# One decoder layer on one core: the third output tile's weights split by halves, and turned attention probabilities copied bank by bank on two engines

## The chip, the cores and the metric

The kernel runs on one core of a Trainium2 chip. The metric is the device time of one execution in microseconds. Times of instructions come from one profiled execution, counted from its first instruction.

## What is computed

One layer of a hybrid decoder for 1024 tokens of width 1024, all in float32:

```python
h = rmsnorm(x, norm1_w)
proj = h @ w_in                       # columns are shared out between two mixers
o_a = gated_delta_rule(...)           # 4 heads of 128, after a short causal convolution
o_b = dilated_attention(qb, kb, vb)   # 8 heads of 64; three (window, dilation) branches
x = x + concat(o_a, o_b) @ w_out      # one output projection
h = rmsnorm(x, norm2_w)
u = causal_dwconv(h @ w_up, ffn_conv_w)
x = x + (silu(u[:, :2816]) * u[:, 2816:]) @ w_down
return rmsnorm(x, final_norm_w)
```

The attention lets each query see the last 128 keys, every fourth key of the last 512 and every sixteenth of the last 2048.

## The kernel before

**Precision.** A float32 product is made of three products of a reduced type (`mm3`, L196): both operands are split into a high part (a ScalarE copy into the reduced type) and a low part (VectorE subtracts the high part from the original). The products are high × high, high × low and low × high. `split` (L202) makes such a pair; `weight` (L211) takes a raw weight tile of 128 × 1024 (`wst`, loaded by DMA), allots `whi` and `wlo` from rings of two buffers each, and splits it; `wk` (L219) views the two as eight blocks of 128 columns, one for each block of the contraction.

**Order of the work.** The kernel is written as streams (Python generators). A planner, `Weave` (L46 to L118), runs them against a simple model of the engines: each call on VectorE or ScalarE is charged a fixed time and a time per column (L148 to L154), and a stream goes on when the tiles that it asks for (`need`) are ready by that model. So the planner fixes the order of TensorE's list. Dense products of the input projection have a low rank (level 9) and fill the places where other streams would wait. The order on the other engines is fixed when the program is built, by a scheduler that works with priorities. Engine handles `ve` and `ac` have the plain priority of their place in the program; `uv` and `ua` (L151, L152) take the same instructions with a precedence of 400 places (`URGENT`). Helpers record all instructions of these handles under one line: L139 for the plain ones, L141 for those with precedence; L189 is every matmul and L193 every transpose on TensorE.

**Banks.** Matmul results go to PSUM banks of 128 × 512, allotted from rings of two by tag (`asc`, `atr`, `hf`, `ch`).

**Attention** (L892 to L1043). Four pairs of heads, each with eight query blocks of 128, are worked off as 16 pairs of blocks. For a pair, `scores` makes query-key products in two banks for each block: near keys (128 columns for the first block, else 256) and far keys (32 columns for each earlier block before the neighbour, in `far` columns in all). `softmax` finds the minimum of the negated scores on VectorE (`mx`), exponentiates on ScalarE into `sm`, with the sums in `den`. `turn` (L942) transposes the probabilities in pieces of 64 queries: one bank for the first 64 queries, the other for the last 64 (`pvs`, `HALVES`). From each bank the near part (up to 2 heads × 2 × 64 columns) is copied into `pt`, where the two halves lie interleaved, and each far part (2 × 64 columns; none for the first two blocks, one for the next four, two for the last two) into `pb`. Then come the scores of the next pair, which need the same four banks, and `values`, which multiplies `pt` by the values. `rd` is the reciprocal of the sums, on VectorE.

**Output projection** (L1080 to L1120). Eight output tiles of 128 channels, in the order `MORDER` (L1049): 0, 4, 1, 5, 2, 6, 3, 7. The first two are built up together while the mixers' outputs arrive, one in `hf` banks and one in `ch` banks. The others follow one by one, two halves of 24 matmuls each, in `hf` banks. After a tile, VectorE adds its banks to the residual rows `x1` (the profile's `x`); then (L1113 to L1115) the weights of the tile after next are split and its residual rows are loaded, and `residual` (L1142) stores `x1` (to `xpark`) and makes the inputs of the up-projection (`hb`, `B`, `T`) and the sums of squares (`sq`, `rstdB`). DMAs are issued from one queue, SyncE's.

Of the kernel before, what the change touches and what calls it, by code (L numbers as in the profile page):

```python
# [7 lines left out]
F32 = mybir.dt.float32  # L8
F32R = mybir.dt.float32r
AF = mybir.ActivationFunctionType  # L10
OP = mybir.AluOpType
# [4 lines left out]
P = 128  # L16
S = 1024
KT = 8
# [126 lines left out]
def hybrid_layer(tc, I, out):  # L145
# [5 lines left out]
    uv = Engine(wv, nc.vector, "vector", 0.07, 0.00105, first=tc.high_priority)  # L151
    ua = Engine(wv, nc.scalar, "scalar", 0.12, 0.00085, first=tc.high_priority)  # L152
# [4 lines left out]
    wp = es.enter_context(tc.tile_pool(name="wp", bufs=1))  # L157
# [5 lines left out]
    def tile_(pool, shape, dt, name, tag, bufs):  # L163
        return wv.slot(pool.tile(list(shape), dt, name=name, tag=tag, bufs=bufs), tag, bufs)
# [3 lines left out]
    def A(name, tag, dt=F32, shape=(P, 1024)):  # L168
        if tag in TURNS:
            i = turns[tag] = turns.get(tag, -1) + 1  # L170
            tag = TURNS[tag][i % len(TURNS[tag])]
        return tile_(lp, shape, dt, name, tag, SLOTS[tag])
# [19 lines left out]
    def tp(dst, src, idt=None, us=0.11):  # L192
        tc.stamp_issue_order_token(nc.tensor.transpose(dst, src, ident if idt is None else idt).ins, TOKEN)  # L193
        wv.product(us, dst, src)

    def mm3(dst, lhs, rhs, first, last, **kw):  # L196
        us = 0.2135 * rhs[0].shape[-1] / 512
        mm(dst, lhs[0], rhs[0], us, first, False, **kw)
        mm(dst, lhs[0], rhs[1], us, False, False, **kw)
        mm(dst, lhs[1], rhs[0], us, False, last, **kw)  # L200

    def split(src, hi, lo):  # L202
        ac.activation(hi, src, AF.Copy)
        return ve.tensor_tensor(lo, src, hi.bitcast(F32), op=OP.subtract)

    def raw_weight(src, n=1024):
        st = tile_(wp, [P, n], F32, "wst", "wst", 2)
        sy.dma_start(st, src)
        return st

    def weight(src, n=1024, st=None):  # L211
        if st is None:
            st = raw_weight(src, n)
        hi = tile_(wp, [P, n], F32R, "whi", "whi", 2)
        lo = tile_(wp, [P, n], F32R, "wlo", "wlo", 2)
        split(st, hi, lo)
        return hi, lo

    def wk(src, st=None):  # L219
        return [t.rearrange("p (k m) -> p k m", k=KT) for t in weight(src, st=st)]  # L220
# [23 lines left out]
    def bank(tag, name="ps"):  # L244
        return tile_(pp_, (P, 512), F32, name, tag, 2)
# [7 lines left out]
    def half(i):  # L253
        return slice(i * 512, i * 512 + 512)
# [17 lines left out]
    for k in range(KT):  # L272
        xt = A("xt", ("kT*", "dv*")[k % 2])
        xts.append(xt)
        if k % 2 == 0:
            wst = tile_(wp, [P, 2, 384], F32, "wst", "wst", 2)
            whi, wlo = [A(nm, "uy", F32R, (P, 2, 384)) if k < 4 else A(nm, "kt", F32R, (P, 2, 384))
                        for nm in ("whi", "wlo")]
# [611 lines left out]
    HALVES = (slice(0, 64), slice(64, 128))  # L890

    def attention():  # L892
# [49 lines left out]
        def turn(pair):  # L942
            pts = A("pt", "dv*", shape=(P, 2, 2, 256))
            for b, (it, tag) in enumerate(zip(pair, ("asc", "atr"))):
                sm, near, far, u, den = it["sm"], it["near"], it["far"], it["u"], it["den"]
                nn, nf = near // P, -(-far // P)
                pt = it["pt"] = pts[:, b]
                pps = [bank(tag) for _ in range(2)]
                yield wv.need(*pps, sm, slack=TSLACK[b])
                pvs = [pp.rearrange("p (e i t) -> p e i t", e=2, t=64) for pp in pps]  # L950
                for e in range(2):
                    for i in range(nn + nf):
                        o = far + i * P if i < nn else (i - nn) * P
                        for pv, rr in zip(pvs, HALVES):
                            tp(pv[:, e, i, :], sm[rr, e, o:o + P], ident[rr, rr], 0.055)
                for pv, rr in zip(pvs, HALVES):
                    uv.tensor_copy(pt.rearrange("p e (i t) -> p e i t", t=P)[:, :, :nn, rr], pv[:, :, :nn, :])
                    for i in range(nf):
                        rows = min(it["far"] - i * P, P)
                        ua.activation(it["pb"][i][:rows, :, u, rr], pv[:rows, :, nn + i, :], AF.Copy)  # L960
                rd = it["rd"] = tile_(sp, [P, P], F32, "rd", ("r0", "r1", "w0", "w1")[u], 1)
                uv.reciprocal(rd.rearrange("p (e d) -> p e d", e=2), den[:, :, None].to_broadcast([P, 2, 64]))

# [62 lines left out]
        for pi in range(4):  # L1026
            q, k, vn, vc = cur
            for hh in range(2):
# [4 lines left out]
                pb = [A("pb", "qa", shape=(P, 2, 4, P)) for _ in range(1 + hh)]  # L1033
# [15 lines left out]
    MORDER = (0, 4, 1, 5, 2, 6, 3, 7)  # L1049

    def load_residual(m):
        x1[m] = A("x1", "kT")
        sy.dma_start(x1[m], I["xT"][m * P:(m + 1) * P, :])
# [26 lines left out]
    def out_proj():  # L1080
        yield from wv.until("dense")
        ws = [wk(I["wo"][m]) for m in MORDER[:2]]
        yield from wv.until("last group")
        yield from wv.until("residual")
        pts = {}
        todo = [(k, j) for k in range(8) for j in range(2)]
        while todo:

            now = [a for a in todo if ("ot", a[0]) in wv.done and (a[1] == 0 or "attention" in wv.done)]
            if not now:  # L1090
                yield 0.3
                continue
            k, j = now[0]
            todo.remove(now[0])
            m, w = MORDER[j], ws[j]
            if m not in pts:
                pts[m] = [bank(("hf", "ch")[j]) for _ in range(2)]
            for h in range(2):
                yield wv.need(pts[m][h], *w, *ots[k])
                mm3(pts[m][h], [t[:, k, :] for t in w], [t[:, half(h)] for t in ots[k]], k == 0, k == 7)  # L1100
        for j, m in enumerate(MORDER):
            w = ws.pop(0)
            for h in range(2):
                if j > 1:
                    pt = bank("hf")
                    yield wv.need(pt, *w)
                    for k in range(8):
                        mm3(pt, [t[:, k, :] for t in w], [t[:, half(h)] for t in ots[k]], k == 0, k == 7)
                        yield 0.0
                else:  # L1110
                    pt = pts[m][h]
                ve.tensor_tensor(x1[m][:, half(h)], x1[m][:, half(h)], pt, op=OP.add)
            if j + 2 < 8:  # L1113
                ws.append(wk(I["wo"][MORDER[j + 2]]))
                load_residual(MORDER[j + 2])  # L1115
            elif j == 6:
                up_first()
                wv.done.add("last weights")
            residual(m)
        wv.done.add("proj")  # L1120
# [21 lines left out]
    def residual(m):  # L1142

        sy.dma_start(xpark[m], x1[m])
        t = hb[m] = A("hb", "dv")
        for h in range(2):
            ac.activation(t[:, half(h)], x1[m][:, half(h)], AF.Copy, scale=n2[:, m:m + 1])
        i = m % 4
        if m < 4:
            split_block(hblock("B11", i), t[:, half(0)])  # L1150
            t1 = tile_(sp, [P, 512], F32, "t1s", "t2", 2)
            ve.tensor_tensor(t1, t[:, half(1)], t[:, half(0)], op=OP.subtract)
            split_block(hblock("T1", i), t1)
        else:
            (b11, b12), (b21, b22) = [[x[:, half(h)] for h in range(2)] for x in (hb[i], t)]

            ve.tensor_tensor(b12, b22, b12, op=OP.subtract)
            ve.tensor_tensor(b11, b12, b11, op=OP.add)
            split_block(hblock("T2", i), b11)
            split_block(hblock("B21", i), b21)  # L1160
            split_block(hblock("T3", i), b12)
            ve.tensor_tensor(b21, b21, b11, op=OP.subtract)
            split_block(hblock("T4", i), b21)
            split_block(hblock("B22", i), b22)
        for h in range(2):
            sl = half(h)
            sq = tile_(sp, [P, 512], F32, "sq2", "t2", 2)
            ac.activation(rstdB[:, sl] if m == 0 else sq, x1[m][:, sl], AF.Square)
            if m:
                ve.tensor_tensor(rstdB[:, sl], rstdB[:, sl], sq, op=OP.add)  # L1170
# [66 lines left out]
    def up_first():  # L1237
        load_up(0)
        up_weights(0, ("A11", "S1"))
# [271 lines left out]
    for h in range(H):  # L1511
        wv.add(1, chain(h))
    wv.add(5, attention())
    wv.add(8, out_proj())
    wv.add(0, mixer_splits())
    wv.add(8, mlp_up())
# [61 lines left out]
```

## Time and profile before

| | us |
|---|---|
| median of 3 runs | 1223.74 |
| lowest and highest | 1222.77, 1223.82 |
| the profiled execution | 1223.87 |
| its span, first to last instruction | 1222.1 |
| attention on TensorE | about 330 to 460 |
| output projection | about 481 to 570 |
| up-projection, then down-projection | to about 992, then to the end |

In the profile, PE is TensorE's matrix multiplication, PEld its loading of weights, DVE VectorE, ACT ScalarE, SP the DMA queue's engine. A row of a timeline gives the start, the time from start to end, the engine, the line, the operation, the tiles written and read, the shapes and the count, and in brackets the idle time of that engine before it with what ended it. A row of a group gives the count, the busy time in all in us, the mean of one in ns, and the idle time before. Matmuls overlap: a 128 × 512 product is shown as 0.39 us long though the next one starts 0.23 after it.

### The profile page before, as it was taken

The numbers are of one execution on the slowest core, as the hardware profiler recorded it, in microseconds if no ns is written. First come the engines' busy times: TensorE is split into PE (matmuls) and PEld (weight loads), VectorE is DVE, ScalarE is ACT, GpSimd is POOL, SyncE is SP. The second block draws the span as 40 slices with busy tenths as digits, with TensorE's granted clock in tenths as the row PEclk, the third lists the DMA queues.
The fourth block names the chain that finished last, engine by engine and source line by source line (L and its number), as shares of the span: only waits on it lengthen the run. The fifth ranks groups of instructions, "written<-read, shape, count | busy, mean of one in ns | idle before, by whom it ended". The sixth has DMA issues, their size and how long they took to land.

```text
span 1222.1 us, 18237 instructions
## 1 busy us (share of the span) xinstructions
PE 1201.4 (98%) x7064; PEld 986.3 (81%) x7064; DVE 950.3 (78%) x1458; ACT 574.5 (47%) x1123; POOL 50.1 (4%) x46
## 2 busy tenths in 40 slices
PE   9999999999999999999999999999999999999996
PEld 7878887889777778788888888888888888787886
DVE  7675965566487686668988988989889889899875
ACT  7393344356344453555545544445444444343441
POOL 0211010003100000000000000000000000000000
PEclk9999999999999999999999999999999999999998
DMA  7425252335634213444223123132231496555623
GB/s 228 110 74 168 77 148 88 118 126 163 215 105 121 88 37 101 157 147 155 71 68 104 58 98 99 57 104 65 91 101 55 142 369 238 165 164 181 193 81 138
DMA packets 85799, 154.81 MB, mean 127 GB/s; under 512 B 21168, under 2 KB 36304, under 8 KB 85712
## 3 DMA queue, kind: packets, MB, share of 16 engines
q1 hardware_dynamic: 85712, 153.64, 39.3%
q8 instruction: 55, 0.90, 0.3%
q14 instruction: 32, 0.26, 0.1%
HBM read 117.68 MB, written 35.93 MB: 126 GB/s over the span
## 4 chain that ended last, share of the span: by engine, by line
PE 84%; DVE 8%; DMA 3%; issue 2%; ACT 2%; SPq 0%; POOLq 0%; POOL 0%; DVEq 0%; ACTq 0%
PE ps L189 43%; PE pa L189 20%; PE pc L189 10%; PE dw L189 8%; PE ps L193 3%; DMA wd<-in_wd 3%; DVE pr L139 2%; DVE x1h L139 1%; DVE kT L139 1%; DVE wd L139 1%; ACT dec L139 1%; DMA xt<-in_xT 1%; DVE wlo L139 0%; DVE r L139 0%; ACT sq L141 0%
## 5 line engine op out<-in xcount | busy, mean ns | idle before, releaser
L189 PE MATMUL dw<-pr 128*128 128x512 f32 (+1 forms) x984 | 213.4, 378 | 3.3 <-DVE x1h L139 3.1
L189 PEld LDWEIGHTS dw<-pr 128*128 128x128 f32 x984 | 176.2, 188 | 39.5 <-DVE x1h L139 4.8
L189 PE MATMUL ps<-xhi,whi 128*128 128x512 f32 x384 | 158.7, 413 | 0.0
L189 PE MATMUL ps<-xlo,whi 128*128 128x512 f32 x384 | 150.2, 391 | 0.6 <-DVE xlo L139 0.6
L189 PE MATMUL ps<-xhi,wlo 128*128 128x512 f32 x384 | 150.4, 392 | 0.0
L189 PE MATMUL pa<-T,pair 128*128 128x512 f32 x528 | 127.1, 390 | 0.0
L189 PEld LDWEIGHTS pa<-T,pair 128*128 128x128 f32 x528 | 99.0, 188 | 20.5
L189 PEld LDWEIGHTS ps<-xhi,wlo 128*128 128x128 f32 x384 | 72.1, 188 | 15.7 <-DVE wlo L139 0.2
L189 PEld LDWEIGHTS ps<-xhi,whi 128*128 128x128 f32 x384 | 72.3, 188 | 14.9 <-issue 1.4
L189 PEld LDWEIGHTS ps<-xlo,whi 128*128 128x128 f32 x384 | 72.4, 189 | 12.8 <-DVE xlo L139 1.0
L139 ACT ACTIVATE whi<-wst 128x1024 fp32r<-128x1024 f32 (+2 forms) x42 | 42.9, 1023 | 76.8 <-PE ps L189 53.6
L139 ACT ACTIVATE u<-pa 128x512 f32<-128x512 f32 x44 | 26.4, 599 | 109.5 <-PE pa L189 109.5
L139 DVE SCALAR_TENSOR_TENSOR y<-xu,fcw,y 128x1023 f32<-128x1023 f32 (+1 forms) x44 | 56.4, 1281 | 22.1 <-ACT y L139 22.0
L189 PE MATMUL pa<-B,A 128*128 128x512 f32 x264 | 63.4, 389 | 0.0
L189 PE MATMUL pc<-T,S 128*128 128x512 f32 x264 | 63.4, 389 | 0.0
L189 PE MATMUL pc<-B,pair 128*128 128x512 f32 x264 | 63.4, 389 | 0.0
L189 PE MATMUL pa<-T,S 128*128 128x512 f32 x264 | 63.4, 389 | 0.0
L139 DVE TENSOR_TENSOR wst<-wst 128x512 f32<-128x512 f32 x88 | 60.6, 688 | 0.9
L139 DVE TENSOR_TENSOR wlo<-wst,whi 128x1024 fp32r<-128x1024 f32 (+2 forms) x42 | 49.5, 1177 | 14.5 <-ACT whi L139 14.3
L189 PE MATMUL ps<-B,pair 128*128 128x512 f32 x252 | 60.5, 389 | 0.0
L139 ACT ACTIVATE pr<-wd 128x1024 fp32r<-128x1024 f32 x33 | 34.9, 1059 | 54.5 <-DVE wd L139 32.3
L189 PEld LDWEIGHTS pc<-B,pair 128*128 128x128 f32 x264 | 49.6, 188 | 10.3
(241 smaller groups left out, 2341.8 us busy)
## 6 DMA issues: line engine op xcount, KB each, us to landing
wst<-in_wu SPq DMA_DIRECT2D x44, 512.0 KB, 3.6
wd<-in_wd SPq DMA_DIRECT2D x44, 512.0 KB, 4.1
upark<-y SPq DMA_DIRECT2D x22, 512.0 KB, 3.7
wst<-in_wi SPq DMA_DIRECT2D x21, 512.0 KB, 3.7
r<-upark SPq DMA_DIRECT2D x11, 512.0 KB, 8.1
r<-upark SPq DMA_DIRECT2D x22, 256.0 KB, 7.0
wa<-in_wd SPq DMA_DIRECT2D x22, 256.0 KB, 2.8
wst<-in_wv SPq DMA_DIRECT2D x8, 512.0 KB, 3.7
```

Source lines behind the costliest of these rows:

```text
L139: return getattr(eng, op)(*a, **kw)
L189: tc.stamp_issue_order_token(nc.tensor.matmul(dst, lhs, rhs, start=start, stop=stop, **kw).ins, TOKEN)
L193: tc.stamp_issue_order_token(nc.tensor.transpose(dst, src, ident if idt is None else idt).ins, TOKEN)
```

## The change

Two edits. The weights of the third output tile (`j == 0`, so `MORDER[2]`) are split in two halves of 512 columns (four blocks each), first half first, and both engines' instructions take precedence. In `turn`, all copies from the first bank of a block go to VectorE and all copies from the second bank to ScalarE; before, VectorE made the near copies and ScalarE the far copies of both banks.

```diff
+    def wk_by_halves(src):
+        st = raw_weight(src)
+        hi = tile_(wp, [P, 1024], F32R, "whi", "whi", 2)
+        lo = tile_(wp, [P, 1024], F32R, "wlo", "wlo", 2)
+        for h in range(2):
+            sl = half(h)
+            ua.activation(hi[:, sl], st[:, sl], AF.Copy)
+            uv.tensor_tensor(lo[:, sl], st[:, sl], hi[:, sl].bitcast(F32), op=OP.subtract)
+        return [t.rearrange("p (k m) -> p k m", k=KT) for t in (hi, lo)]
...
-                for pv, rr in zip(pvs, HALVES):
-                    uv.tensor_copy(pt.rearrange("p e (i t) -> p e i t", t=P)[:, :, :nn, rr], pv[:, :, :nn, :])
+                copies = uv.tensor_copy, lambda dst, src: ua.activation(dst, src, AF.Copy)
+                for pv, rr, copy in zip(pvs, HALVES, copies):
+                    copy(pt.rearrange("p e (i t) -> p e i t", t=P)[:, :, :nn, rr], pv[:, :, :nn, :])
                     for i in range(nf):
                         rows = min(it["far"] - i * P, P)
-                        ua.activation(it["pb"][i][:rows, :, u, rr], pv[:rows, :, nn + i, :], AF.Copy)
+                        copy(it["pb"][i][:rows, :, u, rr], pv[:rows, :, nn + i, :])
...
-                ws.append(wk(I["wo"][MORDER[j + 2]]))
+                ws.append((wk_by_halves if j == 0 else wk)(I["wo"][MORDER[j + 2]]))
```

## The prediction

> **What bounds the kernel now.** I read the page's busy line first, then who waited for whom on TensorE over the whole span, then the timelines of the two places that the change edits.
>
> ```profile
> PE 1201.4 (98%) x7064; PEld 986.3 (81%) x7064; DVE 950.3 (78%) x1458; ACT 574.5 (47%) x1123; POOL 50.1 (4%) x46
> ```
>
> TensorE is busy 98% of the span, so the kernel gets faster only where TensorE stands still or where its list gets shorter. The change touches no matmul. What it can win is therefore a wait of PE. These are the two waits that bear on it:
>
> ```profile
> PE ps L189 <- DVE wlo L139: 0.8, 1, 0.8
> PE ps L189 <- ACT pb L141: 0.5, 1, 0.5
> ```
>
> Each happened once (us in total, times, longest). The first lies in the output projection, the second in the attention. The timelines show what each costs, since a busy bar hides part of a stall (matmul ends are modelled): I measure from start to start.
>
> ```profile
> 503.93 0.39 PE L189 MATMUL ps<-ohi,wlo 128*128 128x512 f32 x1
> 504.15 0.40 PE L189 MATMUL ps<-ohi,whi 128*128 128x512 f32 x1
> 504.39 0.39 PE L189 MATMUL ps<-olo,whi 128*128 128x512 f32 x1
> 505.55 0.50 PE L189 MATMUL ps<-ohi,wlo 128*128 128x512 f32 x1 [0.77 <-DVE wlo L139]
> 505.89 0.39 PE L189 MATMUL ps<-ohi,whi 128*128 128x512 f32 x1
> ```
>
> The third tile's first product starts at 504.15. Its third product, the first that reads the low weights, should start 0.23 after 504.39, at 504.62; it starts at 505.55: 0.93 us lost. The next one comes 0.34 later where 0.23 is the step: 0.11 more for starting again. 1.04 us in all is what this stall costs.
>
> Why it is late, on VectorE and ScalarE:
>
> ```profile
> 502.31 2.05 DVE L139 TENSOR_TENSOR x<-x,ps 128x512 f32<-128x512 f32 x3 [4.41 <-PE ps L189]
> 504.28 1.22 DVE L139 TENSOR_TENSOR wlo<-wst,whi 128x1024 fp32r<-128x1024 f32 x1
> 502.83 1.06 ACT L139 ACTIVATE whi<-wst 128x1024 fp32r<-128x1024 f32 x1 [5.65 <-PE ps L189]
> ```
>
> The high part can't begin before 502.83, because its buffer is the first tile's, released by PE. It is done at 503.89. By then VectorE has begun its third residual addition (three in 2.05, so 0.68 each, the third from 503.67 to 504.36), and the whole low part follows, until 505.50.
>
> **Part one: the split by halves.** Half-wide rows are in the same stage:
>
> ```profile
> 531.74 0.63 ACT L139 ACTIVATE T<-hb 128x512 fp32r<-128x512 f32 x1 [2.04 <-DVE hb L139]
> 532.28 0.62 ACT L139 ACTIVATE B<-hb 128x512 fp32r<-128x512 f32 x1
> 509.48 0.69 DVE L139 TENSOR_TENSOR hb<-hb 128x512 f32<-128x512 f32 x1
> 510.08 0.69 DVE L139 TENSOR_TENSOR T<-t1s,T 128x512 fp32r<-128x512 f32 x1
> ```
>
> A half costs ScalarE 0.63 and VectorE 0.69; a second one right behind starts 0.54 and 0.60 after the first. So the first high half runs from 502.83 to 503.46. VectorE finishes the second addition at 503.68, and with precedence takes the first low half then, until 504.37, then the second (504.28 to 504.97). Before, 1.22 after the third addition; now PE's first use at 504.62 needs only the first half, 0.25 us ahead of time. The second half is first read by the 15th product (weights are used block by block, four blocks a half), 14 steps of 0.23 after 504.15, at 507.4. The cost: two halves take VectorE 1.29 instead of 1.22, ScalarE 1.17 instead of 1.06. Queued behind on VectorE are the third and fourth additions, which now start at about 504.9 and 505.5; on ScalarE the scaled residual copy. Nobody on PE waits for these within 5 us: the additions free the `ch` banks, while the third tile writes `hf` banks.
>
> [...]
>
> What is late next is a load:
>
> ```profile
> 505.52 0.33 SPq L139 DMA_DIRECT2D wst<-in_wo  x1
> 506.55 3.75 SPq L139 DMA_DIRECT2D x<-in_xT  x1
> 514.72 0.69 DVE L139 TENSOR_TENSOR x<-x,ps 128x512 f32<-128x512 f32 x1 [2.15 <-DMA x<-in_xT]
> 516.13 0.39 PE L189 MATMUL ps<-ohi,whi 128*128 128x512 f32 x1
> ```
>
> The third tile's residual rows are issued at 506.55 and land only just before 514.72; the addition that reads them frees, at 515.41, the bank into which PE writes the fourth tile from 516.13. That is 0.72 us of slack. PE coming 1.04 earlier wants the bank at 515.09. If the landing doesn't move, PE stands until about 515.46 and pays the 0.11 again: net gain 0.56. The load of weights at 505.52 follows the end of `wlo` (505.50) and now goes about 0.5 earlier, ahead of it on the same queue, so the landing may come up to 0.5 earlier, and then all of 1.04 stays. I take −0.8 (from −1.04 to −0.56; +0.1 if VectorE's order stays). All later additions in this projection wait for PE or have microseconds to spare, and the up-projection behind it runs without a gap, so what is won is kept.
>
> **Part two: one bank each.** Today VectorE copies both banks' near parts and ScalarE the far parts, behind VectorE on the same bank:
>
> ```profile
> L141 DVE COPY pt<-ps 128x256 f32<-128x256 f32 x56 | 19.5, 405 | 0.0
> L141 DVE COPY pt<-ps 128x128 f32<-128x128 f32 x8 | 1.9, 282 | 1.3 <-PE ps L193 1.3
> L141 ACT ACTIVATE pb<-ps 128x128 f32<-128x128 f32 x24 | 6.6, 275 | 6.2 <-DVE pt L141 5.8
> ACT pb L141 <- DVE pt L141: 18.9, 14, 2.1
> L141 ACT ACTIVATE sm<-sm,mx 128x256 f32<-128x256 f32 x8 | 4.0, 496 | 0.2 <-DVE mx L141 0.2
> ```
>
> (The fourth line is from the view of waits, from 330 to 470.) VectorE gives away 28 copies of 256 columns at 19.5/56 = 0.35 and 4 of 128 at 1.9/8 = 0.24, 10.8 us, and takes 32 far copies at no more than 0.24, 7.7: 3.1 us less. ScalarE gives away 32 far copies at 0.275, 8.8, and takes 32 near ones. No row has ScalarE copying 256 columns from a bank: it lies between the 0.275 of 128 columns and the 0.496 of an exponential over 256. I take 0.45, by the nearer row: about 13.7 in, so 5 us more. [...] Either is hidden unless the banks come free later than PE asks. In a regular pair they don't:
>
> ```profile
> 371.01 0.96 PE L193 MATMUL ps<-ident,sm 64*128 64x64 f32 x24
> 374.85 1.38 PE L189 MATMUL ps<-kT,qT 64*128 64x256 f32 x16
> 372.52 1.26 ACT L141 ACTIVATE pb<-ps 32x128 f32<-32x128 f32 x4 [1.30 <-DVE pt L141]
> ```
>
> Turned by 371.97, copied by 373.78, wanted at 374.85: 1.07 us to spare, filled with dense products. Faster copies win nothing here. ScalarE's share for the pair is 4 copies, at most 2 × (0.50 + 0.27) = 1.54 from 371.5 on; even a 1.05 us weight copy in front leaves it done by 374.1. Two pairs are late:
>
> ```profile
> 390.52 0.49 PE L189 MATMUL ps<-kT,qT 64*128 64x128 f32 x4
> 391.53 1.03 PE L189 MATMUL ps<-kT,qT 64*128 64x256 f32 x4 [0.52 <-ACT pb L141]
> 392.49 1.09 PE L189 MATMUL ps<-pt,vn 128*64 128x128 f32 x16
> 427.09 0.93 PE L189 MATMUL ps<-kT,qT 64*128 64x128 f32 x8
> 427.95 0.66 PE L189 MATMUL ps<-pt,vn 128*64 128x128 f32 x8
> 389.46 1.22 DVE L139 TENSOR_TENSOR wlo<-wst,whi 128x1024 fp32r<-128x1024 f32 x1
> 390.59 0.75 DVE L141 COPY pt<-ps 128x256 f32<-128x256 f32 x2
> 391.05 0.76 ACT L141 ACTIVATE pb<-ps 128x128 f32<-128x128 f32 x4 [1.04 <-DVE pt L141]
> 360.12 1.32 PE L189 MATMUL ps<-kT,qT 64*128 64x128 f32 x8
> 361.38 0.88 PE L189 MATMUL ps<-pt,vn 128*64 128x128 f32 x12
> ```
>
> The same eight score products take 0.86 from start to successor at 427.09, but 1.97 at 390.52 and 1.26 at 360.12: 1.11 and 0.40 lost. At 390.59 a weight's `wlo` stands between the two members' copies. After the change VectorE does one near and two far copies there, 0.35 + 2 × 0.24 = 0.83, from 390.59 to 391.42, if `wlo` stays in between, and ScalarE has finished its own bank before. The first late product then starts perhaps 0.1 earlier and the second, freed today by the last `pb` copy (391.81), 0.3 earlier. If `wlo` goes behind, most of the 1.11 is won. I take −0.4 for both (from −1.5 to +0.5, the latter for a weight copy falling between ScalarE's own copies in a few pairs).
>
> **Sum.** −0.8 − 0.4 = −1.2. The profiled execution took 1223.87 (span 1222.1 and 1.77 around it) and becomes 1222.7; the median of the runs lies 0.13 below the profiled one, so 1222.5.
>
> **Rivals.** (1) *All the stalls go, and a third one with them.*
>
> ```profile
> 339.57 2.01 PE L193 MATMUL ps<-ident,sm 64*128 64x64 f32 x24
> ```
>
> These turns take 2.01 where the same 24 at 371.01 take 0.96: 1.05 lost on exponentials, with no dense product put in front. If the planner, which charges the copies to other engines now, has one ready there, all of it goes: 1.04 + 1.11 + 0.40 + 1.05 = 3.6, so 1220.1. Against it: that wait isn't for the copies. 0.2.
>
> (2) *It doesn't do what it says.* Both banks' copies write interleaved columns of one tile. If the two engines are held apart for that, or the third addition keeps its place before the first low half (low half 504.28 to 504.97, 0.35 after 504.62), part two gives 0 and part one some 0.3 to 0.5: 1223.4. 0.15.
>
> (3) *Slower: more pieces in PE's list.* The planner places dense products by its own estimate of when banks come free; both edits shift that estimate.
>
> ```profile
> 388.24 0.50 PE L189 MATMUL ps<-xhi,whi 128*128 128x512 f32 x1
> 388.57 0.40 PE L189 MATMUL ps<-xlo,whi 128*128 128x512 f32 x1
> ```
>
> After attention products, the first dense step is 0.33 instead of 0.23, and going back costs 0.1 too: each further piece costs 0.2. With one more in each of the 16 pairs that is +3.2, less 0.8 from part one: 1226.1. It decides over the sign from 6 more pieces on (6 × 0.2 = 1.2). For it: the estimate decides by thresholds. Against it: the estimate chains the four near copies through the one tile they write, whoever makes them, at nearly equal prices (0.339 and 0.338), so few thresholds should flip. 0.15.
>
> **How the numbers follow.** My forecast has 0.5, the rivals 0.2, 0.15 and 0.15. A difference within 0.2% (2.4 us) is about what a measurement of this kernel can tell from no change: forecast and rival 2 lie within it, so same 0.65, faster 0.2, slower 0.15. The range goes from rival 1 at 1220.0 to 1225.0, past the +0.5 and +0.1 of the two parts and half of rival 3.
>
> **What would show it.** Right: PE's wait for `wlo` gone in the projection, two low halves before the third addition; a new short wait of PE near 515 for the residual addition, or a landing before 514.6; ScalarE's 18.9 us behind `pt` gone. Wrong: PE's list in the attention in another order, `wlo` still last at 505, or a stall of over 1 us at a pair that has none today.

## The result, and the profile after

| | before | after |
|---|---|---|
| median of 9 runs each, us | 1223.71 | 1220.63 |
| lowest to highest, us | 1222.03 to 1224.93 | 1219.28 to 1222.81 |
| the profiled execution and its span, us | 1223.87, 1222.1 | 1219.28, 1217.5 |

The ratio of the changed kernel's time to that of before is 0.9981, with a 95% interval from 0.9973 to 0.9989: 2.3 us faster (1.3 to 3.3 by the interval), where the prediction's sum was 1.2. The two medians lie 3.1 apart, but the nine executions of one kernel spread over 2.9 and 3.5 us, so a median is not good to a microsecond. Both parts of the change did what they say, and each was worth more than forecast.

To see where the time came from I cut both traces at four marks of TensorE's list and took the starts of the products there: the first product of the attention's scores, the first of the third output tile, the first of the up-projection and the first of the down-projection.

| stage, us | before | after | difference |
|---|---|---|---|
| start to the first score product | 329.84 | 328.75 | -1.09 |
| first score product to the third output tile | 174.31 | 172.99 | -1.32 |
| third output tile to the up-projection | 66.38 | 65.28 | -1.10 |
| up-projection | 421.71 | 421.71 | 0.00 |
| down-projection to the end | 229.86 | 228.76 | -1.10 |

The second stage holds the copies of the turned probabilities, the third the split weights. The first and the last hold nothing that the change touches: there, each engine has the same instructions in the same order in both traces. The experiments show below that these two stages come out differently from one profile to the next. So I count 1.32 + 1.10 = 2.42 us as the changed kernel's own gain, and the other 2.2 of the 4.6 between the two spans as luck of the profiled executions; that of the changed kernel is the fastest of its nine. The ratio agrees with 2.42.

The page's busy line of the changed kernel:

```profile
PE 1200.4 (99%) x7064; PEld 986.3 (81%) x7064; DVE 946.1 (78%) x1459; ACT 574.6 (47%) x1124; POOL 52.1 (4%) x46
```

PE has the same 7064 matmuls and a busy time lower by only 1.0, where the span is 4.6 shorter: most of the gain is time in which PE stood. VectorE has 4.2 us less to do (3.1 forecast).

**The third output tile.** The changed kernel's timeline answers to the stall at 505.55 of before:

```profile
500.42 1.15 ACT L141 ACTIVATE whi<-wst 128x512 fp32r<-128x512 f32 x2 [5.93 <-PE ps L189]
...
501.19 0.69 DVE L141 TENSOR_TENSOR wlo<-wst,whi 128x512 fp32r<-128x512 f32 x1
...
501.74 0.39 PE L189 MATMUL ps<-ohi,whi 128*128 128x512 f32 x1
501.79 0.68 DVE L139 TENSOR_TENSOR x<-x,ps 128x512 f32<-128x512 f32 x1
501.97 0.39 PE L189 MATMUL ps<-olo,whi 128*128 128x512 f32 x1
502.20 0.39 PE L189 MATMUL ps<-ohi,wlo 128*128 128x512 f32 x1
502.39 0.68 DVE L141 TENSOR_TENSOR wlo<-wst,whi 128x512 fp32r<-128x512 f32 x1
502.42 0.39 PE L189 MATMUL ps<-ohi,whi 128*128 128x512 f32 x1
...
502.99 0.68 DVE L139 TENSOR_TENSOR x<-x,ps 128x512 f32<-128x512 f32 x1
503.10 0.33 SPq L139 DMA_DIRECT2D wst<-in_wo  x1
...
504.75 0.33 SPq L139 DMA_DIRECT2D x<-in_xT  x1
...
510.46 0.69 DVE L139 TENSOR_TENSOR x<-x,ps 128x512 f32<-128x512 f32 x1 [0.20 <-DMA x<-in_xT]
```

The four products now start 0.23 apart. VectorE slips the first low half in ahead of the third residual addition and ends it at 501.88, 0.32 before PE asks; the second half goes between the third addition and the fourth. PE's wait for `wlo` is gone. The residual rows' load, which the prediction feared, was in time: its addition ends at 511.15, and PE writes the fourth tile only from 512.62 (10.88 after 501.74).

**The copies.** These are groups of the changed kernel between 329 and 460 (count, busy us, mean ns, idle before):

```profile
L141 DVE COPY pt<-ps 128x256 f32<-128x256 f32 x28 | 11.1, 395 | 0.0
L141 ACT ACTIVATE pt<-ps 128x256 f32<-128x256 f32 x28 | 10.6, 378 | 3.0 <-PE ps L193 2.9
L141 DVE COPY pb<-ps 128x128 f32<-128x128 f32 x12 | 3.3, 273 | 0.0
L141 ACT ACTIVATE pb<-ps 128x128 f32<-128x128 f32 x12 | 3.2, 271 | 0.0
```

The near copies are shared evenly, and ScalarE no longer waits for VectorE's `pt` (before: 18.9 us, 14 times). Before, a bank's far copies came after its near copy: at the late scores of 390.52 the near copies of the second block's two banks ran from 390.59 to 391.34, and ScalarE, after 1.04 of waiting for `pt`, began their far copies at 391.05. Whether two engines could copy from one bank at once no run tests. After, each bank has one engine, and that wait is gone from the view.

The late pair that started at 390.52 before, in the timeline of the changed kernel:

```profile
387.11 0.37 DVE L141 COPY pt<-ps 128x256 f32<-128x256 f32 x1
387.18 0.36 ACT L141 ACTIVATE pt<-ps 128x256 f32<-128x256 f32 x1
387.38 0.46 DVE L141 COPY pb<-ps 128x128 f32<-128x128 f32 x2
387.44 0.41 ACT L141 ACTIVATE pb<-ps 128x128 f32<-128x128 f32 x2
387.77 1.20 DVE L139 TENSOR_TENSOR wlo<-wst,whi 128x1024 fp32r<-128x1024 f32 x1
388.77 1.68 PE L189 MATMUL ps<-kT,qT 64*128 64x128 f32 x8
388.90 0.41 DVE L141 COPY pt<-ps 128x256 f32<-128x256 f32 x1
389.24 0.47 DVE L141 COPY pb<-ps 128x128 f32<-128x128 f32 x2
...
390.39 1.09 PE L189 MATMUL ps<-pt,vn 128*64 128x128 f32 x16
```

ScalarE is done with both of its banks at 387.85. VectorE still has a weight's `wlo` between the two members, so its second bank comes free at 389.71, and the eight score products take 1.62 from start to successor: 0.35 less than the 1.97 of before, but still 0.76 more than the 0.86 that they need. The other late pair runs from 358.91 to 359.77, 0.86: all of its 0.40 is won.

That is 0.75 of the 1.32. The rest comes from pairs that the prediction had not looked at: the scores of the last two blocks of each of the four pairs of heads, which need the banks of the two blocks before. First before, then after:

```profile
380.32 1.00 DVE L139 TENSOR_TENSOR oT<-ps,rT 128x512 f32<-128x512 f32 x1
381.17 1.39 DVE L141 COPY pt<-ps 128x256 f32<-128x256 f32 x4
381.61 1.26 ACT L141 ACTIVATE pb<-ps 96x128 f32<-96x128 f32 x4 [1.70 <-DVE pt L141]
...
382.35 2.03 PE L189 MATMUL ps<-kT,qT 64*128 64x256 f32 x40
```

```profile
380.47 0.27 DVE L141 COPY pb<-ps 128x128 f32<-128x128 f32 x1
380.73 1.89 PE L189 MATMUL ps<-kT,qT 64*128 64x256 f32 x40
```

There VectorE first scales a finished output (`oT`, 1.00) and then made four near copies, and ScalarE's last far copy, bound to them, ended at 382.87, half a microsecond after PE had begun the scores. Now VectorE's last copy ends at 380.74, as PE begins, and the same 40 score products take 1.89 instead of 2.03. The same order stands ahead of the scores of last blocks in all four pairs of heads, and together they give 0.56. That `oT` is what makes these four late is read from the rows; no run moved it.

### The profile page after: what moved, and what is told of

Same layout as the page of the kernel before. It is cut to its first block, busy times and chain, and to the rows that moved or that the text cites. A ratio compares the mean times of both kernels' runs of the same rounds, so it can differ in the third digit from the quotient of the medians.

```text
span 1217.5 us, 18285 instructions
## 1 busy us (share of the span) xinstructions
PE 1200.4 (99%) x7064; PEld 986.3 (81%) x7064; DVE 946.1 (78%) x1459; ACT 574.6 (47%) x1124; POOL 52.1 (4%) x46
## 4 chain that ended last, share of the span: by engine, by line
PE 87%; DVE 6%; DMA 3%; issue 2%; ACT 2%; SPq 0%; POOLq 0%; POOL 0%; DVEq 0%; ACTq 0%
PE ps L189 44%; PE pa L189 20%; PE pc L189 10%; PE dw L189 10%; PE ps L193 3%; DMA wd<-in_wd 2%; DVE pr L139 2%; DVE x1h L139 1%; DVE wd L139 1%; DVE kT L139 1%; ACT dec L139 1%; PE warm L189 1%; DVE wlo L139 0%; DMA r<-upark 0%; ACT sq L141 0%
## 5 line engine op out<-in xcount | busy, mean ns | idle before, releaser
L141 ACT ACTIVATE sm<-sm,mx 128x128 f32<-128x128 f32 (+7 forms) x64 | 35.4, 555 | 60.0 <-DVE mx L141 60.0
```

What stands on the lines that cost most here:

```text
L141: return getattr(eng, op)(*a, **kw)
```

## The experiments

Theory A: each part does what its code says, and each removes waits of PE for operands or banks; the two gains add up; what the planner's list does is worth nothing. The rivals: that the changed list (rival 3 of the prediction, or its opposite) moves the time; that precedence, not the halves, brings the low half forward; that the two parts share a gain. The first four kernels ran together on one chip, the next four together on another, and their ratios are to runs of the kernel before beside them.

| kernel | ratio to before, 95% interval | score to third tile, us | third tile to up-projection, us |
|---|---|---|---|
| the kernel before | 1 | 174.31 | 66.38 |
| the changed kernel | 0.9981 [0.9973, 0.9989] | 172.99 | 65.28 |
| split only | 0.9992 [0.9983, 1.0001] | 174.32 | 65.28 |
| banks only | 0.9988 [0.9979, 0.9997] | 172.95 | 66.39 |
| list only | 1.0002 [0.9993, 1.0011] | 174.37 | 66.33 |
| banks, old list | 0.9988 [0.9979, 0.9997] | 172.99 | 66.36 |
| halves, no precedence | 0.9988 [0.9979, 0.9997] | 174.33 | 65.28 |
| precedence, no halves | 0.9999 [0.9990, 1.0008] | 174.29 | 66.37 |
| second tile split too | 0.9977 [0.9967, 0.9986] | 172.68 | 65.28 |
| and a gap filled | 0.9962 [0.9948, 0.9976] | 171.63 | 65.28 |

The stages tell more than the ratios here: two executions of the same lists agree in them to 0.1, while a ratio's interval is 2 us wide.

**Split only.** The changed kernel with the copies of before.

```diff
-                copies = uv.tensor_copy, lambda dst, src: ua.activation(dst, src, AF.Copy)
-                for pv, rr, copy in zip(pvs, HALVES, copies):
-                    copy(pt.rearrange("p e (i t) -> p e i t", t=P)[:, :, :nn, rr], pv[:, :, :nn, :])
+                for pv, rr in zip(pvs, HALVES):
+                    uv.tensor_copy(pt.rearrange("p e (i t) -> p e i t", t=P)[:, :, :nn, rr], pv[:, :, :nn, :])
...
-                        copy(it["pb"][i][:rows, :, u, rr], pv[:rows, :, nn + i, :])
+                        ua.activation(it["pb"][i][:rows, :, u, rr], pv[:rows, :, nn + i, :], AF.Copy)
```

> The kernel before with the third tile's weights split by halves with precedence; turn as before. Stages are measured on TensorE from start to start: from the first score product to the third output tile's first product 174.31 us before and 172.99 after the whole change; from there to the first up-projection product 66.38 and 65.28. Theory A (the two edits are two separate stalls and add up): the second stage falls to 65.3, the first stays at 174.3; the whole is 1.1 us shorter than before. Rival B (the projection comes out shorter because the attention changed the arrival of its inputs): the second stage stays near 66.4. Rival C (part of the gain lies in the down-projection, 229.86 before and 228.76 after, and is caused by the change): the down-projection falls by 1.1 as well.

**Banks only.** The changed kernel with every weight split whole.

```diff
-                ws.append((wk_by_halves if j == 0 else wk)(I["wo"][MORDER[j + 2]]))
+                ws.append(wk(I["wo"][MORDER[j + 2]]))
```

> The kernel before with the turned banks copied one by VectorE and one by ScalarE; the third tile's weights in one piece. Theory A: the stage from the first score product to the third tile's first product falls from 174.31 to 173.0 and the stage behind it stays at 66.4; the whole is 1.3 us shorter. Rival B: the second stage falls too, to about 65.3. Rival C: the down-projection falls by 1.1.

Of these two stages the split shortens only its own, by 1.10, and the banks only theirs, by 1.36; their sum is the changed kernel's 2.42 within 0.04, and rival B has fallen. The ratios, 0.9992 and 0.9988, agree with 1.1 and 1.4 of 1223 us, but their intervals alone could not have told the one part from the other.

Rival C is not settled as clearly. The down-projection did come out 1.11 shorter in split only (228.75) and unchanged in banks only (229.82), as it would if the split caused it. But list only, with neither edit, had 227.89, and second tile split too, with the split, had 229.66. If the split were worth 2.2 in all, its ratio would be 0.9982, just outside the interval of split only. So I leave the down-projection out of the gain.

**List only.** The kernel before, with the planner charged for the copies as in the changed kernel: each copy runs where it did, but the handle charges the other engine.

```diff
+    uv_as_a = Engine(wv, nc.vector, "scalar", 0.12, 0.00085, first=tc.high_priority)
+    ua_as_v = Engine(wv, nc.scalar, "vector", 0.07, 0.00105, first=tc.high_priority)
...
-                for pv, rr in zip(pvs, HALVES):
-                    uv.tensor_copy(pt.rearrange("p e (i t) -> p e i t", t=P)[:, :, :nn, rr], pv[:, :, :nn, :])
+                for pv, rr, vec, act in zip(pvs, HALVES, (uv, uv_as_a), (ua_as_v, ua)):
+                    vec.tensor_copy(pt.rearrange("p e (i t) -> p e i t", t=P)[:, :, :nn, rr], pv[:, :, :nn, :])
...
-                        ua.activation(it["pb"][i][:rows, :, u, rr], pv[:rows, :, nn + i, :], AF.Copy)
+                        act.activation(it["pb"][i][:rows, :, u, rr], pv[:rows, :, nn + i, :], AF.Copy)
```

> The kernel before with every instruction on its old engine, but the planner charges the copies as the change does, so that TensorE's list is that of the kernel after (a triple of dense products before instead of behind the scores of a pair, at two pairs). Theory A (two thirds of the attention's gain is banks freed earlier in two late pairs, one third is these two moved triples, 0.27 us each): the stage from the first score product to the third tile is 173.8, 0.5 below 174.31. Rival D (the division of the banks wins nothing, the planner's list is all): 173.0. Rival E (the moved triples only hide elsewhere): 174.3.

**Banks, old list.** The reverse: the copies of the changed kernel, charged as before, and no split.

```diff
-                copies = uv.tensor_copy, lambda dst, src: ua.activation(dst, src, AF.Copy)
-                for pv, rr, copy in zip(pvs, HALVES, copies):
-                    copy(pt.rearrange("p e (i t) -> p e i t", t=P)[:, :, :nn, rr], pv[:, :, :nn, :])
+                copies = ((uv.tensor_copy, uv_as_a.tensor_copy),
+                          [lambda dst, src, e=e: e.activation(dst, src, AF.Copy) for e in (ua_as_v, ua)])
+                for pv, rr, (copy_near, copy_far) in zip(pvs, HALVES, copies):
+                    copy_near(pt.rearrange("p e (i t) -> p e i t", t=P)[:, :, :nn, rr], pv[:, :, :nn, :])
...
-                        copy(it["pb"][i][:rows, :, u, rr], pv[:rows, :, nn + i, :])
+                        copy_far(it["pb"][i][:rows, :, u, rr], pv[:rows, :, nn + i, :])
```

> The turned banks are copied one by VectorE and one by ScalarE, but the planner charges the copies as before, so that TensorE's list is that of the kernel before; weights in one piece. Theory A: the stage from the first score product to the third tile is 173.5, 0.8 below 174.31, won at the pairs whose scores were late (1.97 us for eight score products at 390.52 and 1.26 at 360.12, against 0.86 elsewhere). Rival D: 174.3.

The list does change: at two pairs three dense products stand ahead of the scores that stood behind them before. Alone it is worth nothing (174.37 against 174.31), and the copies alone give the whole gain (172.99, where 173.5 was expected). Where the expectation counted a gain for each moved triple, it was wrong. In this kernel, whose list is that of before row for row, the gain can be read pair by pair, from one pair's first score product to the next pair's: 0.40 and 0.36 at the two late pairs, 0.13 to 0.15 at each of the four pairs of last blocks, and under 0.04 at all others together.

**Halves, no precedence.** The kernel before, with the halves on the plain handles.

```diff
-                ws.append(wk(I["wo"][MORDER[j + 2]]))
+                ws.append((wk_by_halves if j == 0 else wk)(I["wo"][MORDER[j + 2]]))
...
-            ua.activation(hi[:, sl], st[:, sl], AF.Copy)
-            uv.tensor_tensor(lo[:, sl], st[:, sl], hi[:, sl].bitcast(F32), op=OP.subtract)
+            ac.activation(hi[:, sl], st[:, sl], AF.Copy)
+            ve.tensor_tensor(lo[:, sl], st[:, sl], hi[:, sl].bitcast(F32), op=OP.subtract)
```

(The second pair of lines stands against the changed kernel's function.)

> The kernel before, with the third tile's weights split by halves on the plain handles, without precedence. Theory A (the halves alone shorten the way to the first low block; the scheduler's order puts a low half ahead of the third addition by itself, since a half's turn in the program is met by then): from the third tile's first product to the first up-projection product 65.3 us, as with precedence (65.28), not 66.4; no wait of PE for wlo at the third tile. Rival (it is the precedence that lets the low half pass the third addition): the low half comes 0.68 later, the stall is 0.5 to 0.7 and the stage 65.8 to 66.0. Ratio to the kernel before 0.9991 by the theory, 0.9996 by the rival.

Its timeline:

```profile
502.61 0.69 DVE L139 TENSOR_TENSOR wlo<-wst,whi 128x512 fp32r<-128x512 f32 x1
...
503.21 0.69 DVE L139 TENSOR_TENSOR x<-x,ps 128x512 f32<-128x512 f32 x1
...
503.62 0.39 PE L189 MATMUL ps<-ohi,wlo 128*128 128x512 f32 x1
503.81 0.69 DVE L139 TENSOR_TENSOR wlo<-wst,whi 128x512 fp32r<-128x512 f32 x1
```

**Precedence, no halves.** The kernel before, with the third tile's weights split whole on the handles with precedence (the changed function with one pass over all 1024 columns).

> The kernel before, with the third tile's weights split whole (1024 wide) but with precedence. Theory A: no order changes, since the high part waits for its buffer and the whole low part for it; VectorE has begun the third addition by then. The same 66.4 us from the third tile's first product to the first up-projection product, and 174.3 from the first score product to the third tile. Ratio 1.0000, so it also shows how far two executions of the same lists lie apart: the start up to the first score product within 328.7 to 329.9, the down-projection within 227.8 to 229.9. Rival (precedence wins by itself): the low part passes the third addition, 0.1 less.

```profile
504.27 1.22 DVE L141 TENSOR_TENSOR wlo<-wst,whi 128x1024 fp32r<-128x1024 f32 x1
...
505.54 0.50 PE L189 MATMUL ps<-ohi,wlo 128*128 128x512 f32 x1 [0.77 <-DVE wlo L141]
```

The halves do all of it. On the plain handles VectorE's order is the same, low half ahead of the third addition, and the stage is 65.28 again; precedence alone leaves the stall of 0.77 in its place. The likely reason, which no run tests: the whole high part ends only after the third addition has begun, without precedence (503.89 and 503.67 before) as with it (503.88 and 503.67 here).

**Second tile split too.** The changed kernel still has a smaller stall of the same kind at the second output tile, so I carried the cure there.

```diff
-        ws = [wk(I["wo"][m]) for m in MORDER[:2]]
+        ws = [f(I["wo"][m]) for f, m in zip((wk, wk_by_halves), MORDER)]
```

> The changed kernel, with the second tile's weights split by halves with precedence as well. In the changed kernel PE's first product with the second tile's low weights, near 481.7, starts 0.42 late, and the next 0.11 late. Theory A (a stall of PE for a low part goes with the halves and all of it is kept): from the first output product to the third tile's first product 22.0 instead of 22.48, and the rest of the stages as in the changed kernel (172.99 from the first score product to the third tile's becomes 172.5; 65.28 behind it). Ratio to the kernel before 0.9977. Rival (the stall near 480.2 for the bank of the second result sets this place, or the halves' 0.07 more on VectorE delay the additions): 22.4 to 22.6, ratio 0.9981.

The changed kernel's timeline, then this one's:

```profile
480.38 1.23 DVE L139 TENSOR_TENSOR wlo<-wst,whi 128x1024 fp32r<-128x1024 f32 x1 [0.22 <-ACT whi L139]
...
481.24 0.40 PE L189 MATMUL ps<-olo,whi 128*128 128x512 f32 x1
...
481.66 0.50 PE L189 MATMUL ps<-ohi,wlo 128*128 128x512 f32 x1
```

```profile
481.11 1.28 DVE L141 TENSOR_TENSOR wlo<-wst,whi 128x512 fp32r<-128x512 f32 x2
...
482.28 0.39 PE L189 MATMUL ps<-olo,whi 128*128 128x512 f32 x1
...
482.51 0.39 PE L189 MATMUL ps<-ohi,wlo 128*128 128x512 f32 x1
```

The stall went, and 0.31 of the stage with it (172.99 to 172.68), not 0.5. My expectation had taken the step of 0.42 for the loss; the loss is what the step has over 0.23, so 0.19, and 0.10 for starting again.

**And a gap filled.** Beside that, `values` is put off until its tile is due by the planner's model, so that the list has dense products where PE stood for the first exponentials with far keys (the prediction's 339.57).

```diff
             yield wv.need(pair[0]["po"], pair[0]["pt"], slack=-PSLACK)
+            yield wv.need(pair[0]["vn"], slack=-4.0)
```

> The kernel of the run before, with one more condition for the planner: it puts values off until the values' tile is due by its model (with 4 us allowed early). The list then holds two triples of dense products between the scores of the first pair of blocks with far keys and its values, where PE stood for the exponentials (the transposes that took 2.01 instead of 0.96, 1.05 lost), and one triple more at a later pair; three triples fewer follow that. Theory A (a stall of PE on the exponentials is filled by dense products that must be made anyway, less 0.2 for each further piece in the list): from the first score product to the third tile's first product 0.65 to 0.85 less than in the run before, so 171.6 to 171.9. Ratio to the kernel before 0.9970. Rival (the exponentials come as much later as the dense products take, or the added pieces cost what they fill): 172.3 to 172.6, ratio 0.9977.

The turns of that pair in the changed kernel, then in this one:

```profile
338.49 2.01 PE L193 MATMUL ps<-ident,sm 64*128 64x64 f32 x24
```

```profile
341.17 0.96 PE L193 MATMUL ps<-ident,sm 64*128 64x64 f32 x24
...
359.54 1.20 DVE L139 TENSOR_TENSOR wlo<-wst,whi 128x1024 fp32r<-128x1024 f32 x1
360.54 1.69 PE L189 MATMUL ps<-kT,qT 64*128 64x128 f32 x8
...
391.01 0.47 DVE L141 COPY pb<-ps 128x128 f32<-128x128 f32 x2
391.84 0.93 PE L189 MATMUL ps<-kT,qT 64*128 64x128 f32 x8
```

The gap is filled: the stage is 1.05 shorter than in the run before (171.63 against 172.68), more than the 0.65 to 0.85 expected, and this is the fastest kernel of the study by its stages and its median (1217.79, five runs; the interval of its ratio overlaps that of the run before). It shows another thing by accident. The dense products moved, and with them the weights' splits on VectorE: `wlo` no longer falls between the copies of the pair at 391.84 (0.86 from start to successor, 0.76 less than in the changed kernel) but between those of the pair at 360.54 (1.61, 0.75 more). At either pair a `wlo` between the two members goes with the same loss of 0.75, and the pair without it has none. That stall is still there to be won; it wasn't tried.

## Why the prediction was half right

The sign and the order of size held, both mechanisms worked where the prediction looked for them, and 1220.63 lies inside the range. The sum of 1.2 was half of the 2.42 that the stages show, and 0.56 of that came from pairs for which the prediction had put nothing. The median lies nearer to rival 1 (1220.1) than to the forecast (1222.5), and that is luck: rival 1's third stall did not go, and the medians lie 0.7 further apart than the stages account for. By its own steps:

- **Part one, -0.8: the mechanism right, the size -1.10.** The stall's 1.04 went whole, and 0.05 more: nine other steps next to it were 0.229 to 0.236 before, and are 0.227 after. The step that failed is the trim for the residual load ("The third tile's residual rows are issued at 506.55 and land only just before 514.72"). That addition began 10.57 after the third tile's first product in the one execution that I had; in four other kernels without the split, 8.45 to 10.06; in the five with it, 8.43 to 9.41. PE asks for the bank at 10.88, less 0.69 for the addition, so only the first of all these would have cost anything. I had taken the latest landing for the rule. That the load would be issued earlier was wrong too: the weights' load ahead of it came 1.37 after that product before and 1.36 after, since the second low half now ends behind the third addition. "Two low halves before the third addition" was wrong in order, and harmless.
- **Part two, -0.4: -1.32.** Two terms. The two late pairs gave 0.40 and 0.36, where I had put 0.4 for both: the pair at 360.12 won all, the pair at 390.52 a third of its 1.11, because `wlo` stayed between, as the text allowed. And "Faster copies win nothing here" was read from one pair and held for all others; it fails in the four pairs of last blocks, 0.56 together, where `oT` stands ahead of the copies.
- **The near copy, 0.45.** It took 0.378 in the mean, and the far copy began 0.27 after it (386.60 to 386.87). So the estimate from the two rows was 0.07 too high. ScalarE's busy time stayed as it was, 574.5 and 574.6, instead of rising by 5; nothing hung on it.
- **What the halves cost.** The two halves did take VectorE longer: 0.69 and 0.68, with the third addition between them, against 1.22, so 0.15 more, where the prediction had them back to back in 1.29. The stage came out 1.10 shorter all the same: PE did not need the whole low part by then, but its first half.
- **Rival 1** fell: the transposes' 2.01 stayed (338.49). It was right that the place could be filled; the last experiment did. **Rival 2** fell: the engines write `pt` at the same time (387.11 and 387.18), and the first low half passed the third addition. **Rival 3** was right that the list changes, at two pairs, and wrong on its price: 0.

What stays open: why the start and the down-projection vary where no edit reaches (below).

## What to carry over

Where one engine prepares an operand for another in one long instruction, ask when the first piece is read, not when the last is done: halves back to back took the two engines 0.15 us more here (1.15 for 1.06 on ScalarE, and 1.28 for 1.22 on VectorE at the second tile) and won PE 1.10 at the third tile, and a precedence without them won nothing. Before you write that a faster step "wins nothing", go through every repetition of it with its start-to-successor time; a stage of 16 pairs had six that were late, and I had found two. A margin taken from one execution's DMA landing is one sample; don't trim a sum with it.

## What the runs showed of the hardware

- One queue in one order gave landings up to 2.1 us apart. In the five profiles without the split the weights' load was issued 1.36 or 1.37 after the third tile's first product, the residual load behind it 2.4 to 3.8 after, and the addition that needs it began 8.45 to 10.57 after. The residual load's own row lasted 3.75 us in the profile before, 2.73 in list only and 0.33 to 0.37 in the other three; the late issues were not the late landings (banks only: issued 3.8 after, addition 8.55 after). The lateness is there already in the weights' load ahead on the queue: from issue to landing it took 6.6 us before, 6.1 in precedence, no halves, 5.5 in list only, and 4.3 and 4.2 in the two with the early additions. What decides that stays open.
- Up to the first score product every engine has the same instructions in the same order in all ten traces, and again from about 519 us on. Yet the start took from 328.75 to 330.06 and the down-projection from 227.60 to 229.87. Each range is as large as either part of the change, so the whole span of one profile can't measure one. The up-projection took 421.71 in every kernel.
- After a wait between 128 × 512 products, PE's next step was 0.33 to 0.34 instead of 0.23 in each such stall quoted here (505.55, 505.54, 481.66), and the tenth went with the stall.

Most of the start's difference is one wait. Before, then after:

```profile
69.65 0.66 PE L193 MATMUL ps<-ident,kT 128*128 128x128 f32 x4 [0.91 <-ACT sq L141]
```

```profile
68.58 0.66 PE L193 MATMUL ps<-ident,kT 128*128 128x128 f32 x4
```

In the seven profiles with a start of 329.60 or more this wait was 0.91 to 1.05; in the three with 328.88 or less it was 0.17 at most. In the down-projection TensorE's wait for VectorE's `x1h` was 1.6 to 3.2 in all, 3.1 before and 2.2 after, and the two shortest stages (227.60 and 227.89) had 1.6 each. What moves these waits stays open.
